# Delta-rule triangular solve as 64x64 products on quarters of the TensorE array, with TensorE's work of the delta stage in a written order

## Chip, cores, metric

One Trainium2 chip, one core. The metric is the device time of one execution in microseconds (us); the time shown of a kernel is the median of its runs.

## What is computed

A two-layer transformer-like block on 256 latent tokens and 256 context tokens of width 1024, in float32: modulation and norm, one input projection, three token mixers side by side (a gated convolution, a gated delta rule run in both directions, attention in a window of 128), an output projection, and a channel mixer: a dense SwiGLU in layer 0, a mixture of 8 experts in layer 1. The change touches the delta rule, which has 6 heads of 64 and runs over chunks of 64 tokens:

```python
a_mat = jnp.where(strict, jnp.einsum('bhcid,bhcjd->bhcij', kb, k) * decay, 0.0)
lmat = a_mat + jnp.eye(DN_CHUNK, dtype=F32)
rhs = jnp.concatenate([v * beta[..., None], kb * jnp.exp(gcum)[..., None]], axis=-1)
sol = lax.linalg.triangular_solve(lmat, rhs, left_side=True, lower=True, unit_diagonal=True)
...
v_new = u_c - jnp.einsum('bhik,bhkv->bhiv', w_c, s)
o = jnp.einsum('bhik,bhkv->bhiv', qg_c, s) + jnp.einsum('bhij,bhjv->bhiv', qk_c, v_new)
s = s * gl_c[..., None, None] + jnp.einsum('bhik,bhiv->bhkv', kd_c, v_new)
```

## The kernel before, in words

`layer` runs twice. In each layer `in_proj` makes the projections tile by tile; on the way `dn_gates` makes the gates (`sb` holds beta and -beta for each token and head), and `dn_units` cuts the delta rule into 8 units: a stream (context first, then latent), a direction, and a block of 128 tokens, which is two chunks of 64. For each pair of units `diag_inverse` inverts the 32x32 diagonal blocks of the triangular matrix, row by row, on VectorE for one direction and on GpSimd for the other, and writes the result to scratch in DRAM (`drz`, L1015).

`deltanet` is the delta stage. For each unit there are three parts:

- `dn_front` repeats the decay factors over heads (`headrep`, L769), for a block that is new also transposes keys and values and makes the key-query products (`dn_block`, L854 and L808), and builds the right-hand side `R` (L834, L835) and the operands `QD` (L838, L844).
- `dn_solve` reads the inverse `ud` from DRAM (L877, on SyncE's queue, two buffers), copies the off-diagonal blocks into `B` (L881, ScalarE), and makes three products (`prod`, L891): X = ud*R, then R = R - B*X, then Z = (ud*R)*beta. Each product has 6 matmuls, one for each head, of a 128x128 stationary tile that holds the two chunks as 64x64 blocks on its diagonal (the rest is zeros) and 128 columns. Three heads fill one PSUM tile; VectorE or ScalarE empties it (L896, L898; L900; L902).
- `dn_back` makes from Z the transition `gl` (L925, L934), `bb` (L931, L936), `er` (L943, L945), then the states of the two chunks one after the other (L961, L963) and the output (L972, L979, L985). `need_o` is false for the context in layer 1, whose output nobody needs: L943, L972 and L979 are left out there.

In layer 0 the matmuls of three modulation vectors (`mod_steps`, L316, weights of 1 MB each on SyncE's queue) are spread over the stage. The loop of `deltanet` issues front of unit i, back of unit i-1, solve of unit i and two steps of the modulation; a scheduler of the framework then puts the instructions of every engine and every queue into a static order by priority and by its own estimates, so matmuls of one product are often split and mixed with others, and work of the attention behind the stage (`mix_rest`) can come in front. PSUM has 8 banks; in this stage the tags f, b, c, x, m have 2, 2, 1, 2 and 1.

A matmul in float32 shows as two instructions in the trace: a product of 6 matmuls is a row of x12, one of 12 matmuls a row of x24.

Of the kernel before, what the change touches and what calls it, by code (L numbers as in the profile page):

```python
# [19 lines left out]
P = 128  # L20
# [147 lines left out]
class Build:  # L168
# [319 lines left out]
    def layer(self, l):  # L488
# [169 lines left out]
    def dn_gates(self, l, A):  # L658
# [20 lines left out]
        nc.vector.tensor_scalar(sb[:, :, :, 1], beta, -1.0, None, op0=OP.mult)  # L679
        pg = self.ps("p")  # L680
# [7 lines left out]
        self.D = dict(g=g, beta=beta, sb=sb, eg=eg)  # L688
# [21 lines left out]
    def deltanet(self, l):  # L710
# [8 lines left out]
        mods = itertools.chain(*[self.mod_steps(*m, "m") for m in self.MODS[l]])  # L719
        per = 2  # L720
        for i in range(9):
            if i < 8:
                self.dn_front(units[i])
            if i:
                self.dn_back(units[i - 1])
            if i < 8:
                self.dn_solve(units[i])
            for _ in range(per):
                next(mods, None)
        for _ in mods:  # L730
            pass
    def mix_rest(self, l, n, A, op):
# [3 lines left out]
        if l and not self.stop:  # L736
            self.router_open("m")
# [3 lines left out]
        if not self.stop == f"mix{l}":  # L741
            self.out_part(l, n, 0, [A["oc"][:, i] for i in range(2)] + [A["od"][:, i] for i in range(3)], op, "cm")
# [69 lines left out]
    def dn_front(self, U):  # L812
# [11 lines left out]
        pev = pe[:, :384].rearrange("p (a i) -> p a i", a=3)  # L824
        U["erl"] = dp.tile([P, 3, 2], F, name="erl", bufs=4)
        nc.scalar.activation(U["erl"], pev.rearrange("p q (c i) -> p q c i", c=2)[:, :, :, 0 if d else 63], AF.Copy)
        if need_o:
            U["er"] = dp.tile([P, 3, P], F, name="er", bufs=2)
            nc.vector.tensor_tensor(U["er"], pev, qk[:, :, 1, tk], op=OP.mult)
        if blk not in self.shared:  # L830
            self.shared[blk] = self.dn_block(A, tk, need_o)
# [14 lines left out]
    def dn_block(self, A, tk, need_o):  # L846
# [3 lines left out]
        out = []  # L850
        for i, src in enumerate((A["qk"][:, :, 0], A["v"])):
# [7 lines left out]
            else:  # L859
                nc.vector.tensor_copy(out[i], pv)  # L860
        kq = None
# [6 lines left out]
        return out + [kq]  # L868

    def dn_solve(self, U):  # L870
# [5 lines left out]
        R, ud, B = U["R"], dp.tile([P, 6, P], F, name="ud", bufs=2), self.bo[d]  # L876
        nc.sync.dma_start(ud, U["inv"])  # L877
# [6 lines left out]
        hs = [slice(0, 3), slice(3, 6)]  # L884

        def prod(lhs, rhs):
            for hh in hs:
                p = self.ps("b")
                v = p[:, :384].rearrange("p (a b) -> p a b", a=3)
                for i, m in enumerate(range(hh.start, hh.stop)):  # L890
                    nc.tensor.matmul(v[:, i, :], lhs[:, m, :], rhs[:, m, :], start=True, stop=True)  # L891
                yield v

        for hh, v in zip(hs, prod(ud, R)):
            if hh.start:
                nc.scalar.activation(X[:, hh, :], v, AF.Copy)  # L896
            else:
                nc.vector.tensor_copy(X[:, hh, :], v)  # L898
        for hh, v in zip(hs, prod(B, X)):
            nc.vector.tensor_tensor(R[:, hh, :], R[:, hh, :], v, op=OP.subtract)  # L900
        for i, (hh, v) in enumerate(zip(hs, prod(ud, R))):
            nc.vector.tensor_tensor(  # L902
                Z[:, hh, :].rearrange("p a (u k) -> p a u k", u=2), v.rearrange("p a (u k) -> p a u k", u=2),
                D["sb"][:, blk, d * 6 + 3 * i:d * 6 + 3 * i + 3, :][:, :, :, None].to_broadcast([P, 3, 2, 64]),
                op=OP.mult)

    def dn_back(self, U):
# [19 lines left out]
        for pr in range(3):  # L927
            for c in range(2):
                for par in range(2):
                    m = 2 * pr + par  # L930
                    nc.tensor.matmul(pbv[half[par], pr, c, :], qd[:, m, P + 64 * c:P + 64 * c + 64], Z[:, m, 0:64],  # L931
                                     start=pr == 0 and c == 0, stop=True, skip_group_check=True)
        glf = gl.rearrange("p a c k -> p a (c k)")
# [3 lines left out]
        if need_o:  # L937
# [7 lines left out]
            nc.vector.tensor_tensor(er, prv, er, op=OP.add)  # L945

        states = {}
        for c in ((1, 0) if d else (0, 1)):
# [7 lines left out]
            else:  # L956
# [6 lines left out]
                nc.vector.tensor_tensor(new, psv, bb[:, :, c, :], op=OP.add)  # L963
            self.st[d] = new
# [826 lines left out]
```

## Time and profile before

| | |
|---|---|
| median of 3 runs | 2018.47 us (2017.98 to 2021.39) |
| the profiled execution | 2015.34 us, span 2013.5 us, mean granted TensorE clock 0.974 |
| TensorE busy | 1907.0 us, 95% of the span |
| VectorE busy | 936.7 us, 47% |
| ScalarE busy | 577.4 us, 29% |
| GpSimd busy | 236.7 us, 12% |
| delta stage of layer 0, first to last solve | 220.4 to 323.4 us |
| delta stage of layer 1, first solve to the end of the last unit | 978.5 to 1071.5 us |

How to read it: the share of an engine over the span mixes stages with different limits. The first 1070 us hold projections, the two delta stages, attention and the dense layer; from then on the weights of the experts stream in. What the change is worth is read in the two delta stages, and then in whether the later stages pass it on.

### The profile page before, as it was taken

The page shows a single profiled execution, that of the slowest core. Times are in us where ns is not written, and L with a number is a line of the kernel's source. Part 1 is how long each engine was busy: PE and PEld are TensorE (multiplying, and loading weights), DVE is VectorE, ACT ScalarE, POOL GpSimd, SP SyncE. Part 2 cuts the span into 40 slices and gives each one's busy share as a digit, 9 for nine tenths or more (in the row PEclk, how much of TensorE's full clock was granted, in tenths as well). Part 3 has the DMA queues.
Part 4 walks back from the last instruction along what each step waited for, and adds up shares of the span by engine and source line. Part 5 has one row for each costly group of instructions (what it writes and reads, how often), then busy time and mean ns, then how long its engine had stood idle before and what let it go on. Part 6 is the DMA issues. An engine that isn't in the chain of part 4 may idle for free. (4 is left out here: it accounts for less than half of the span.)

```text
span 2013.5 us, 42986 instructions
## 1 busy us (share of the span) xinstructions
PE 1907.0 (95%) x17677; PEld 1476.4 (73%) x17677; DVE 936.7 (47%) x1862; ACT 577.4 (29%) x1075; POOL 236.7 (12%) x378
## 2 busy tenths in 40 slices
PE   6998999989999999898899999999999999999996
PEld 4776777667888888677786757885688767778853
DVE  3696665677655533577776411111012555521012
ACT  3742223453222223643225300000002354510001
POOL 1165101010000000034700000000000222200000
PEclk9999999999999999898899899999999999999998
DMA  7544453145445423235205799999999999999993
GB/s 302 161 99 108 141 172 131 48 164 188 155 169 209 167 79 105 79 80 142 63 25 207 286 409 408 407 406 408 401 407 406 403 406 406 400 408 397 391 408 135
DMA packets 186543, 497.79 MB, mean 247 GB/s; under 512 B 64864, under 2 KB 83424, under 8 KB 173792
## 3 DMA queue, kind: packets, MB, share of 16 engines
q1 hardware_dynamic: 186336, 494.94, 66.2%
q8 instruction: 141, 2.31, 0.5%
q14 instruction: 66, 0.54, 0.1%
HBM read 485.96 MB, written 8.91 MB: 246 GB/s over the span
## 5 line engine op out<-in xcount | busy, mean ns | idle before, releaser
L437 ACT ACTIVATE wh<-w 128x1024 fp32r<-128x1024 f32 (+4 forms) x162 | 141.6, 887 | 379.9 <-PE psx L467 196.7
L1655 PE MATMUL psx<-r,Xb 128*32 128x128 f32 x2016 | 227.8, 273 | 0.0
L1652 PE MATMUL psx<-r,Xb 128*32 128x384 f32 x2016 | 225.0, 487 | 1.4 <-DVE xs L1072 0.9
L438 DVE TENSOR_TENSOR wl<-w,wh 128x1024 fp32r<-128x1024 f32 (+4 forms) x162 | 163.0, 1014 | 118.1 <-ACT wh L437 117.7
L1655 PEld LDWEIGHTS psx<-r,Xb 128*32 128x32 f32 x2016 | 217.3, 110 | 0.6
L466 PE MATMUL psx<-xh,wh 128*128 128x512 f32 (+1 forms) x384 | 137.6, 387 | 13.0 <-ACT xh L437 8.0
L466 PE MATMUL psx<-fxh,wh 128*128 128x512 f32 x352 | 138.1, 394 | 4.9 <-ACT fxh L437 4.9
L468 PE MATMUL psx<-xh,wl 128*128 128x512 f32 (+1 forms) x384 | 131.8, 373 | 8.8 <-DVE wl L438 8.7
L467 PE MATMUL psx<-fxl,wh 128*128 128x512 f32 x352 | 137.5, 391 | 0.0
L468 PE MATMUL psx<-fxh,wl 128*128 128x512 f32 x352 | 137.3, 390 | 0.0
L467 PE MATMUL psx<-xl,wh 128*128 128x512 f32 (+1 forms) x384 | 132.9, 374 | 0.2 <-DVE xl L438 0.2
L1535 PE MATMUL psx<-r,Xb 128*64 128x256 f32 (+1 forms) x1792 | 130.9, 327 | 1.7 <-issue 1.7
L1732 ACT ACTIVATE hm<-psx 128x256 f32<-128x256 f32 (+3 forms) x63 | 26.2, 416 | 370.2 <-PE psx L1655 203.8
L1501 POOL TENSOR_TENSOR wlo<-r,whi 128x512 fp32r<-128x512 f32 x42 | 57.7, 1374 | 582.1 <-DMA r<-md 411.1
L1501 DVE TENSOR_TENSOR wlo<-r,whi 128x512 fp32r<-128x512 f32 x126 | 104.2, 857 | 44.0 <-ACT whi L1499 32.5
L1535 PEld LDWEIGHTS psx<-r,Xb 128*64 128x64 f32 (+1 forms) x1792 | 87.3, 123 | 41.6 <-issue 8.4
L1687 PE MATMUL psy<-r,hT 128*32 128x256 f32 (+1 forms) x672 | 112.7, 326 | 0.0
L1499 ACT ACTIVATE whi<-r 128x512 fp32r<-128x512 f32 x168 | 99.9, 630 | 42.5 <-PE psx L1508 21.2
L1684 PE MATMUL psy<-r,hT 128*32 128x384 f32 x1008 | 112.1, 486 | 0.0
L1772 PE MATMUL psy<-r,hT 128*32 128x256 f32 (+1 forms) x784 | 104.1, 472 | 1.5 <-DMA r<-md 0.8
L1733 DVE TENSOR_TENSOR hm<-hm,psx 128x256 f32<-128x256 f32 (+3 forms) x63 | 29.4, 466 | 148.5 <-PE psx L1655 75.8
L466 PEld LDWEIGHTS psx<-xh,wh 128*128 128x128 f32 x384 | 73.9, 199 | 29.6 <-ACT xh L437 8.9
(403 smaller groups left out, 3597.0 us busy)
## 6 DMA issues: line engine op xcount, KB each, us to landing
r<-mg SPq DMA_DIRECT2D x224, 512.0 KB, 10.1
r<-mu SPq DMA_DIRECT2D x224, 512.0 KB, 10.1
r<-md SPq DMA_DIRECT2D x224, 512.0 KB, 10.1
wm<-wmod SPq DMA_DIRECT2D x32, 1024.0 KB, 6.2
w<-win SPq DMA_DIRECT2D x24, 1024.0 KB, 5.5
w<-wgu SPq DMA_DIRECT2D x22, 1024.0 KB, 4.9
w<-wmod SPq DMA_DIRECT2D x16, 1024.0 KB, 6.9
w<-wdn SPq DMA_DIRECT2D x16, 704.0 KB, 4.0
```

The lines of the kernel that those rows point to most:

```text
L437: nc.scalar.activation(hi, src, AF.Copy)
L438: nc.vector.tensor_tensor(lo, src, hi.bitcast(F), op=OP.subtract)
L466: nc.tensor.matmul(out, wh[:, k, :], xh[:, k, :n], start=start and k == 0, stop=False)
L467: nc.tensor.matmul(out, wh[:, k, :], xl[:, k, :n], start=False, stop=False)
L468: nc.tensor.matmul(out, wl[:, k, :], xh[:, k, :n], start=False, stop=stop and k == kn - 1)
L1501: eng.tensor_tensor(wl, src, wh.bitcast(F), op=OP.subtract)
L1535: nc.tensor.matmul(out[m * j:m * j + m, :], x[:, k, :], w[k // 2][:, k % 2 * 512 + j * fw:k % 2 * 512 + (j + 1) * fw], start=k == 0, stop= ...
L1652: nc.tensor.matmul(out[32 * g:32 * g + 32], x[:, k, 32 * g:32 * g + 32], w[k // 2][:, c:c + 384], start=k == 0, stop=k == KT - 1, skip_gro ...
L1655: nc.tensor.matmul(out[96:, g * P:(g + 1) * P], x[:, k, 32 * g:32 * g + 32], w[k // 2][:, c + 384:c + 512], start=k == 0 and g == 0, stop= ...
L1684: nc.tensor.matmul(py[half][32 * g:32 * g + 32, :384], lhs[g], w[ft][:, 384 * half:384 * half + 384], start=first, stop=last, skip_group_c ...
L1687: nc.tensor.matmul(py[half][96:, o:o + n], lhs[g], w[ft][:, 768 + c:768 + c + n], start=first and o == 0, stop=last, skip_group_check=True)
L1772: nc.tensor.matmul(py[0][m * dq:m * dq + m, :dw], lhs, w[ft][:, dq * dw:(dq + 1) * dw], start=q == 0 and ft == 0, stop=q == 6 and ft == 3, ...
```

## The change

The two chunks of a head are no longer put on the diagonal of a 128x128 tile with zeros beside them. Each product has 12 matmuls of 64x64 stationary tiles with 128 columns. Even heads (`par` 0) use the quarters of the array whose rows and columns agree, odd heads (`par` 1) the two others, so that four successive matmuls address four different quarters. Even heads write one PSUM tile, odd heads another. For odd heads the result stands with the two chunks exchanged; `B` of odd heads is stored so that the second product exchanges them back, and Z is brought back in the multiplication with beta, by two instructions of 64 partitions with an exchanged copy of the factors, `sx`. The copies into `B` become four in place of two.

TensorE's order in `deltanet` is now the order of the code: in round i a step of the solve of unit i, one of the back of unit i-1 and one of the front of unit i+1 in turns, with two modulation steps in between. The other engines and the queues stay with the scheduler. `ud` is read in the front of a unit in place of its solve. PSUM's tag m is gone, its users take x (the modulation, the router's constants) or c (the output projection), and c has two banks.

```diff
@@ layer @@
-                with self.pool(f"at{l}", 2) as self.ap, self.psum(f"psx{l}", f=2, b=2, c=1, x=2, m=1):
+                with self.pool(f"at{l}", 2) as self.ap, self.psum(f"psx{l}", f=2, b=2, c=2, x=2):
@@ dn_gates @@
+        sx = one([4, 12, 2], "sx")
+        for c in range(2):
+            nc.vector.tensor_copy(sx[64 * c:64 * c + 64], sb[64 - 64 * c:128 - 64 * c])
@@ deltanet @@
-        mods = itertools.chain(*[self.mod_steps(*m, "m") for m in self.MODS[l]])
-        per = 2
-        for i in range(9):
-            if i < 8:
-                self.dn_front(units[i])
-            if i:
-                self.dn_back(units[i - 1])
-            if i < 8:
-                self.dn_solve(units[i])
-            for _ in range(per):
-                next(mods, None)
-        for _ in mods:
-            pass
+        mods = itertools.chain(*[self.mod_steps(*m, "x") for m in self.MODS[l]])
+        with self.tc.manual_schedule(engines={mybir.EngineType.PE}):
+            for i in range(-1, 9):
+                jobs = [f(units[j]) for f, j in ((self.dn_solve, i), (self.dn_back, i - 1), (self.dn_front, i + 1))
+                        if 0 <= j < 8]
+                more = 2
+                while jobs:
+                    jobs = [j for j in jobs if next(j, self) is not self]
+                    if more:
+                        next(mods, None)
+                        more -= 1
+            for _ in mods:
+                pass
@@ dn_front @@
+        U["ud"] = dp.tile([P, 6, P], F, name="ud", bufs=2)
+        nc.sync.dma_start(U["ud"], U["inv"])
...
-            U["er"] = dp.tile([P, 3, P], F, name="er", bufs=2)
+            U["er"] = dp.tile([P, 3, P], F, name="er", bufs=3)
...
+        yield
@@ dn_solve @@
-            p0 = 64 * c + BS * d
             o = BS * (1 - d)
-            nc.scalar.activation(B[p0:p0 + BS, :, 64 * c + o:64 * c + o + BS], U["at"][p0:p0 + BS, :, o:o + BS], AF.Copy)
+            for par in range(2):
+                p0, p1 = 64 * c + BS * d, 64 * (c ^ par) + BS * d
+                nc.scalar.activation(B[p1:p1 + BS, par::2, 64 * c + o:64 * c + o + BS], U["at"][p0:p0 + BS, par::2, o:o + BS],
+                                     AF.Copy)
...
-                for i, m in enumerate(range(hh.start, hh.stop)):
-                    nc.tensor.matmul(v[:, i, :], lhs[:, m, :], rhs[:, m, :], start=True, stop=True)
+            for pr in range(3):
+                for par in range(2):
+                    for c in range(2):
+                        i = half[c ^ par] if back else half[c]
+                        o = half[c] if back else half[c ^ par]
+                        m = 2 * pr + par
+                        nc.tensor.matmul(ps[par][o, pr, :], lhs[i, m, half[c]], rhs[i, m, :], start=pr == 0, stop=True,
+                                         skip_group_check=True)
...
+        for par, v in enumerate(prod(ud, R, False)):
+            sb = D["sx" if par else "sb"][:, blk, d * 6 + par:d * 6 + 6:2, :]
+            for c in range(1 + par):
+                i, o = (half[1 - c], half[c]) if par else (slice(0, P), slice(0, P))
+                n = 64 if par else P
+                nc.vector.tensor_tensor(
+                    Z[o, par::2, :].rearrange("p a (u k) -> p a u k", u=2), v[i].rearrange("p a (u k) -> p a u k", u=2),
+                    sb[i][:, :, :, None].to_broadcast([n, 3, 2, 64]), op=OP.mult)
```

How the orders move. The first place is TensorE in layer 0, solve of unit 3 (`psb`) with the back of unit 2 (`psc`) around it; before:

```order
L769 MATMUL psf<-cnorm,eg 64x128 x6
L925 MATMUL psc<-QD_1822,X 64x128 x6
L891 MATMUL psb<-R,ud 128x128 x4
L931 MATMUL psc<-X,QD_1822 64x64 x12
L891 MATMUL psb<-R,ud 128x128 x2
L891 MATMUL psb<-X,B_1816 128x128
L943 MATMUL psc<-QD_1822,X 64x128 x6
L891 MATMUL psb<-X,B_1816 128x128 x4
L961 MATMUL psc<-st_2004,gl 64x64 x6
L891 MATMUL psb<-X,B_1816 128x128
L891 MATMUL psb<-R,ud 128x128 x2
```

and now (L904 is the product, L944, L950, L963 and L982 are the former L925, L931, L943 and L961, L773 is the former L769):

```order
L904 MATMUL psb<-R,ud 64x128 x12
L944 MATMUL psc<-QD_1825,X 64x128 x6
L950 MATMUL psc<-X,QD_1825 64x64 x12
L773 MATMUL psf<-cnorm,eg 64x128 x6
L316 MATMUL psx<-w,sc 32x256 x8
L904 MATMUL psb<-X,B_1819 64x128 x12
L963 MATMUL psc<-QD_1825,X 64x128 x6
L861 MATMUL psf<-cnorm,tqk 128x128 x3
L316 MATMUL psx<-w,sc 32x256 x8
L904 MATMUL psb<-R,ud 64x128 x12
L982 MATMUL psc<-st_2156,gl 64x64 x6
```

Each product is one piece where it had been two or three, and the work between two products is fixed.

The second place is SyncE's queue in layer 1: the reads of the inverse (`ud`) of the 8 units and the writes of the last two inverses (`drz<-tt`). Before, and now:

```order
L877 DMA ud<-drz_530 128x6x128
L877 DMA ud<-drz_531 128x6x128
L877 DMA ud<-drz_530 128x6x128
L1015 DMA drz_533<-tt 48x16x32 x2
L1015 DMA drz_532<-tt 48x16x32 x2
L877 DMA ud<-drz_531 128x6x128
L877 DMA ud<-drz_532 128x6x128
```

```order
L830 DMA ud<-drz_533 128x6x128
L830 DMA ud<-drz_534 128x6x128
L1037 DMA drz_536<-tt 48x16x32
L1037 DMA drz_535<-tt 48x16x32 x2
L1037 DMA drz_536<-tt 48x16x32
L830 DMA ud<-drz_533 128x6x128
L830 DMA ud<-drz_534 128x6x128
L830 DMA ud<-drz_535 128x6x128
```

The third read, that of unit 2, stood ahead of the four writes and now stands behind them.

The third place is TensorE in layer 1, from the third product of unit 1 on; now:

```order
L904 MATMUL psb<-X,B_8142 64x128 x12
L982 MATMUL psc<-st_8337,gl 64x64 x6
L904 MATMUL psb<-R,ud 64x128 x24
L944 MATMUL psc<-QD_8146,X 64x128 x6
L950 MATMUL psc<-X,QD_8146 64x64 x12
```

The row of x24 is the third product of unit 1 and the first of unit 2, one behind the other; the back of unit 1 and all that follows stand behind them.

## Rows read from the trace of the kernel before

**Rows 1.** The page: busy time of the engines, and GB/s in 40 slices.
```profile
PE 1907.0 (95%) x17677; PEld 1476.4 (73%) x17677; DVE 936.7 (47%) x1862; ACT 577.4 (29%) x1075; POOL 236.7 (12%) x378
...
GB/s 302 161 99 108 141 172 131 48 164 188 155 169 209 167 79 105 79 80 142 63 25 207 286 409 408 407 406 408 401 407 406 403 406 406 400 408 397 391 408 135
```

**Rows 2.** Busy time by stretch, layer 0: us, engines, PEclk, DMA share, GB/s.
```profile
220.40:244.40 24.00, 24.00 (x267) 17.86 (x266) 19.16 (x41) 6.46 (x16) 1.09 (x2) 1.00 0.42 144
...
272.70:302.40 29.70, 29.70 (x386) 22.60 (x385) 22.20 (x47) 6.41 (x15) 0.83 (x1) 1.00 0.45 143
...
sum 103.00, PE 103.00 PEld 80.92 DVE 64.71 ACT 21.29 POOL 5.82; mean PE 25.75 PEld 20.23 DVE 16.18 ACT 5.32 POOL 1.46
```
(The five times are those of PE, PEld, DVE, ACT and POOL.)

**Rows 3.** The same view, layer 1: the start of the stage, and its units.
```profile
965.00:972.50 7.50, 0.54 (x5) 0.30 (x3) 6.84 (x19) 2.12 (x6) 6.87 (x14) 0.72 0.36 105
972.50:978.50 6.00, 5.99 (x31) 5.38 (x31) 1.74 (x4) 1.01 (x2) 5.92 (x9) 0.50 0.01 4
978.50:996.20 17.70, 17.49 (x160) 14.69 (x159) 13.72 (x35) 5.62 (x15) 14.43 (x32) 0.90 0.09 24
996.20:1015.90 19.70, 19.70 (x217) 16.50 (x216) 11.29 (x25) 5.02 (x13) 2.07 (x3) 1.00 0.36 81
1015.90:1036.10 20.20, 20.20 (x238) 17.04 (x237) 18.52 (x40) 6.13 (x14) 0.83 (x1) 1.00 0.08 21
```

**Rows 4.** TensorE in order of time, layer 0: start us, length, engine, line, tiles.
```profile
230.41 0.94 PE L808 MATMUL psf<-tqk 64*128 64x128 f32 x12
231.28 0.71 PE L891 MATMUL psb<-R,ud 128*128 128x128 f32 x4
...
255.45 0.83 PE L925 MATMUL psc<-QD,X 128*64 128x128 f32 x12
256.20 1.16 PE L891 MATMUL psb<-R,ud 128*128 128x128 f32 x8
257.29 0.92 PE L931 MATMUL psc<-X,QD 128*64 128x64 f32 x24
...
265.69 1.93 PE L316 MATMUL psm<-w,sc 128*32 128x256 f32 x32
267.55 0.65 PE L769 MATMUL psf<-cnorm,eg 128*64 128x128 f32 x6
...
272.71 1.60 PE L891 MATMUL psb<-R,ud 128*128 128x128 f32 x12
274.25 1.50 PE L316 MATMUL psm<-w,sc 128*32 128x256 f32 x24
...
283.17 0.92 PE L979 MATMUL psc<-er,st 64*64 64x64 f32 x24
284.01 0.63 PE L316 MATMUL psm<-w,sc 128*32 128x256 f32 x6
```

**Rows 5.** Groups of VectorE, 220.4 to 323.4 us: count, busy us, mean ns, idle before.
```profile
L900 DVE TENSOR_TENSOR R<-R,psb 128x384 f32<-128x384 f32 x16 | 8.8, 553 | 4.1 <-PE psb L891 3.7
L844 DVE TENSOR_TENSOR QD<-kq,E 64x384 f32<-64x384 f32 x16 | 8.8, 552 | 0.7 <-PE psc L972 0.4
L902 DVE TENSOR_TENSOR X<-psb,sb 128x384 f32<-128x384 f32 x15 | 8.4, 557 | 4.7 <-PE psb L891 4.3
```

**Rows 6.** SyncE's queue in layer 1: in time, its wait, and time to landing of `ud`.
```profile
995.85 2.28 SPq L1015 DMA_DIRECT2D drz<-tt  x4
998.24 37.28 SPq L877 DMA_DIRECT2D ud<-drz  x5
...
SPq L1015 <- POOL tt L1011: 8.8, 1, 8.8
...
DMA to landing us min/median/max: 3.3/3.6/6.4
```

**Rows 7.** TensorE in order of time, layer 1, around unit 2's first product.
```profile
994.77 0.94 PE L891 MATMUL psb<-R,ud 128*128 128x128 f32 x6
...
996.21 0.71 PE L891 MATMUL psb<-R,ud 128*128 128x128 f32 x4
```

More of the change, by code (lines that the diff above doesn't have):

```diff
@@ L687, in dn_gates @@
         nc.scalar.activation(eg, pg[:, :96].rearrange("p (k b h) -> p k b h", k=4, b=4), AF.Exp)
[L688 removed]
+        self.D = dict(g=g, beta=beta, sb=sb, sx=sx, eg=eg)
     def dn_units(self, l, A):
@@ L736, in mix_rest @@
         if l and not self.stop:
-            self.router_open("m")
+            self.router_open("x")
         for i, tag in enumerate(tags):
@@ L741, in mix_rest @@
         if not self.stop == f"mix{l}":
-            self.out_part(l, n, 0, [A["oc"][:, i] for i in range(2)] + [A["od"][:, i] for i in range(3)], op, "cm")
+            self.out_part(l, n, 0, [A["oc"][:, i] for i in range(2)] + [A["od"][:, i] for i in range(3)], op, "c")
     def dn_output(self, l, n, A):
@@ L827, in dn_front @@
         if need_o:
-            U["er"] = dp.tile([P, 3, P], F, name="er", bufs=2)
+            U["er"] = dp.tile([P, 3, P], F, name="er", bufs=3)
             nc.vector.tensor_tensor(U["er"], pev, qk[:, :, 1, tk], op=OP.mult)
+        yield
         if blk not in self.shared:
-            self.shared[blk] = self.dn_block(A, tk, need_o)
+            self.shared[blk] = []
+            yield from self.dn_block(A, tk, need_o, self.shared[blk])
         kn, vn, kq = self.shared[blk]
@@ L844, in dn_front, with dn_block @@
                 nc.vector.tensor_tensor(qd[half[c], :, half[c]], kq[half[c]], U["E"][half[c]], op=OP.mult)
-    def dn_block(self, A, tk, need_o):
+    def dn_block(self, A, tk, need_o, out):
         nc, dp, M = self.nc, self.dp, self.M
         half = [slice(0, 64), slice(64, P)]
-        out = []
         for i, src in enumerate((A["qk"][:, :, 0], A["v"])):
@@ L860, in dn_block @@
                 nc.vector.tensor_copy(out[i], pv)
+            yield
         kq = None
@@ L867, in dn_block @@
                     nc.vector.tensor_copy(dst, src)
-        return out + [kq]
+            yield
+        out.append(kq)
     def dn_solve(self, U):
@@ L875, in dn_solve @@
         half = [slice(0, 64), slice(64, P)]
-        R, ud, B = U["R"], dp.tile([P, 6, P], F, name="ud", bufs=2), self.bo[d]
-        nc.sync.dma_start(ud, U["inv"])
+        R, ud, B = U["R"], U["ud"], self.bo[d]
         for c in range(2):
-            p0 = 64 * c + BS * d
             o = BS * (1 - d)
-            nc.scalar.activation(B[p0:p0 + BS, :, 64 * c + o:64 * c + o + BS], U["at"][p0:p0 + BS, :, o:o + BS], AF.Copy)
+            for par in range(2):
+                p0, p1 = 64 * c + BS * d, 64 * (c ^ par) + BS * d
+                nc.scalar.activation(B[p1:p1 + BS, par::2, 64 * c + o:64 * c + o + BS], U["at"][p0:p0 + BS, par::2, o:o + BS],
+                                     AF.Copy)
@@ L882, in dn_solve @@
         X = dp.tile([P, 6, P], F, name="X", bufs=3)
         Z = U["Z"] = dp.tile([P, 6, P], F, name="X", bufs=3)
[L884 to L889, printed above, removed]
-                for i, m in enumerate(range(hh.start, hh.stop)):
-                    nc.tensor.matmul(v[:, i, :], lhs[:, m, :], rhs[:, m, :], start=True, stop=True)
-                yield v
@@ L894, in dn_solve, with prod @@
-        for hh, v in zip(hs, prod(ud, R)):
-            if hh.start:
-                nc.scalar.activation(X[:, hh, :], v, AF.Copy)
-            else:
[L898 to L905, printed above, removed]
+        def prod(lhs, rhs, back):
+            ps = [self.ps("b")[:, :384].rearrange("p (a b) -> p a b", a=3) for _ in range(2)]
+            for pr in range(3):
[6 more added lines that the diff above has]
+                                         skip_group_check=True)
+            return ps
@@ new lines, in dn_solve @@
+        for par, v in enumerate(prod(ud, R, False)):
+            if par:
+                nc.vector.tensor_copy(X[:, par::2, :], v)
+            else:
+                nc.scalar.activation(X[:, par::2, :], v, AF.Copy)
+        yield
+        for par, v in enumerate(prod(B, X, True)):
+            nc.vector.tensor_tensor(R[:, par::2, :], R[:, par::2, :], v, op=OP.subtract)
+        yield
+        for par, v in enumerate(prod(ud, R, False)):
+            sb = D["sx" if par else "sb"][:, blk, d * 6 + par:d * 6 + 6:2, :]
[5 more added lines that the diff above has]
+                    sb[i][:, :, :, None].to_broadcast([n, 3, 2, 64]), op=OP.mult)
@@ L932, in dn_back @@
                                      start=pr == 0 and c == 0, stop=True, skip_group_check=True)
+        yield
         glf = gl.rearrange("p a c k -> p a (c k)")
@@ L945, in dn_back @@
             nc.vector.tensor_tensor(er, prv, er, op=OP.add)
+            yield
         states = {}
@@ L963, in dn_back @@
                 nc.vector.tensor_tensor(new, psv, bb[:, :, c, :], op=OP.add)
+                yield
             self.st[d] = new
```

## The prediction

> **What bounds the kernel now.** I read the page first, then busy time by stretch in both delta stages, then TensorE in order of time, and last VectorE's groups and SyncE's queue. The page [rows 1] gives TensorE 95% of the span, but the GB/s slices show two regimes: up to slice 23 traffic is low and irregular, and from slice 24 on it stands at about 400 to 409, the stream of expert weights. The end of the kernel is that stream. What the change gains in a delta stage therefore counts only if the stream starts earlier. Its first buffers lie where the delta stage of layer 1 had its own, so I take a shift of that stage's end as a shift of the kernel's end, one to one.
>
> In layer 0 TensorE is busy for the whole stage, 103.00 us of 103.00, and VectorE for 64.71 [rows 2]. But VectorE is not idle everywhere: in the first two units it works 19.16 of 24.0 us, and 22.20 of 29.7 in the middle, where blocks are new. Layer 1 [rows 3] has the same picture (11.29 of 19.70 in one pair of units, 18.52 of 20.20 in the next), and ahead of it a hole: from 965.0 to 972.5 TensorE works 0.54 us, while GpSimd, busy 6.87 us, finishes an inverse and the memset of `B` that stands behind it. In the next 6 us the granted clock is 0.50 (the lower level, 1.2 GHz), and the mean after that 0.90. The reader is to keep this: a stand of 7 us costs more than 7 us.
>
> **Price of a product.** A product is 12 instructions of 128x128. Twelve in one piece took 1.54 us (272.71 to 274.25), eight took 1.09 (256.20 to 257.29) [rows 4]. The difference gives 0.112 us an instruction, and what is left is 0.19 us for a piece, the price of a change of tile shape. The 24 products of layer 0 are 288 instructions in 50 pieces (counted in the order): 288 x 0.112 + 50 x 0.19 = 42 us, 1.74 each.
>
> After, a product is 24 instructions of 64x64 with 128 columns. No row shows four quarters at once. Three rows bound it [rows 4]: two row halves together, into two banks, 12 in 0.87 us (L808); two column halves together, 12 in 0.75, 0.062 an instruction (L925); four column strips together, 32 instructions of 256 columns in 1.86, that is 0.058 each and 0.029 for 128 columns (L316). If four quarters work as four strips do, a product takes 24 x 0.029 + 0.17 = 0.87 us; if only two work at once, 24 x 0.062 = 1.5. I take 0.87, because both ways of pairing are seen and the new order addresses four quarters in succession. Even heads write one bank from two row halves. A row shows that this does not make instructions wait: L979 uses the two diagonal quarters into one bank, and 24 instructions of 64 columns took 0.84 us, 0.035 each, where one after the other they would take half of 0.112, 0.056 [rows 4]. The Trainium skill, "TensorEngine Tiling (Array Packing)", Restrictions and Gotchas, says the contrary: "Different row tiles cannot access same PSUM bank simultaneously". By that rule the product would stay at 1.5 us and the sum would be rival B's; the L979 row disagrees with it, at least where the two halves write different partitions, as here.
>
> So 1.74 - 0.87 = 0.87 us a product, 2.6 a unit. The written order also joins other pieces: 143 rows on TensorE between first and last solve before, 113 after of which 8 are attention, so 38 fewer; 26 of these are the products', already counted, and 12 x 0.2 = 2.4 us is 0.3 a unit. **2.9 us a unit** in TensorE's own work.
>
> **Added waits.** Before, the scheduler put other work wherever a product had to wait. Now what stands between two products is fixed. Both banks of the second product end together, so the two subtractions of R, 553 ns each [rows 5], run behind it: with some 0.3 us of signalling 1.4 us before the third product can start. Between stand the `er` product (L943 before), some 0.8 us, and in units 0 to 4 a modulation step. Z becomes three VectorE instructions in place of two. Half the partitions cost no less (L844 with 64 partitions 552 ns, L902 with 128 557 [rows 5]), so 0.55 us more a unit, on the path where the back of the unit waits for Z. Covered fully it is 0. Uncovered it is 1.4 for R, 0.85 for X and 3 x 0.55 + 0.3 for Z, 4.2 in all, less the 0.8 that always stands between: 3.4 us. I take 0.9 a unit (the uncovered rest of R, and half of Z's instruction), nearer to zero since every step has work of the back or the front beside it. Net 2.0 us a unit.
>
> **Layer 0.** Units 0 and 1 are near VectorE's bound (19.16 + 1.1 of 24.0), so I allow 2 us for the pair. Units 2 to 7 give 6 x 2.0 = 12. Eight pieces of attention now stand in the stage, and fill waits of units 5 to 7; that is worth some 2.5 us later. Sum -16.5.
>
> **Layer 1.** Here a queue matters. Before, the read of `ud` for unit 2 stands on SyncE ahead of the writes of the last two inverses. Now it stands behind. These writes wait 8.8 us for GpSimd; they are issued from 995.85, and the next read goes out at 998.24 [rows 6]. GpSimd doesn't get faster by this change. So unit 2's `ud` lands no earlier than 998.24 + 3.6 = 1001.8 (median from issue to landing), where unit 2's first product started at 996.21 before, with unit 1's from 994.77 ahead of it [rows 7]. It starts 5.6 us late. Because units 0 and 1 end 2 us earlier, TensorE stands 7 to 8 us: the back of unit 1 and all else is queued behind that product. As the hole at 965 did, such a stand should be followed by 6 us at half clock, which costs another 3: 8.6 us late at unit 3. Of the rest units 3, 6 and 7 gain 2.0 each, the pair in between is near VectorE's bound (18.52 of 20.20) and gains nothing, and attention in waits is again worth 2.5: 8.6 - 6 - 2.5 = 0.
>
> **At nothing.** The two copies of `sx` are 2 small VectorE instructions at the gates, beside projections. The copies into `B` become four: ScalarE works 21.29 of 103.00 us [rows 2], and `B` is filled a unit ahead; without that cover at most 0.7 us a unit. The third `er` buffer and the PSUM tags only take waits away. `ud` in layer 0 is read some 10 us ahead of its use.
>
> **Sum.** -16.5 us. The profiled execution took 2015.34, which gives 1998.8; the median of the runs is 3.1 above it, so I predict **2002.0** for the median. With w for the added waits of a unit the sum is 1.6 - 9 x (2.9 - w): nine units that gain, and 1.6 for all that doesn't depend on it (-2 - 2.5 + 8.6 - 2.5). At w = 0 this is 1994, at w = 1.8 it is 2010: the forecast's own range.
>
> **Rivals.**
>
> *B, two quarters at a time.* If row halves that share a bank do go one after the other, a product takes 1.5 us and a unit gains 3 x 0.24 + 0.3 = 1.0, of which waits take 0.9. Units 0 and 1 gain nothing: -2.5 + 8.6 - 2.5 - 9 x 0.1 = +2.7, 2021. For it: no row shows four quarters. Against it: L979's row.
>
> *C, no stand in layer 1.* If the inverse is finished earlier or the read reaches its place, layer 1 gains 2 + 6 + 2.5 = 10.5 and the time is 1991.5. For it: GpSimd's start may shift, since the stage before was also reordered. Against it: SyncE's order is static, and the writes stand ahead of the read.
>
> *D, slower: VectorE's delays reach TensorE.* In a fixed order each late eviction stops everything behind it, where before the scheduler had another piece at hand. Place: the third product behind the two subtractions, and the back behind Z. It decides once waits exceed 2.7 us a unit, where the formula gives zero; at the 3.4 worked out above it is +6.1, and 2 more as units 0 and 1 gain nothing: 2026.5. For it: VectorE at 80 to 90% in the units with new blocks. Against it: in the others it is near half.
>
> **How the numbers follow.** Forecast 0.63, B 0.10, C 0.13, D 0.14. The range goes from 1987 (C, with part of its waits covered as well) to 2021 (B); it leaves out D, and the ends of the others, 0.2 in all. 0.2% is 4 us. Faster: the forecast, C and a little of B and D, 0.77; the same, most of B and the edge of the forecast, 0.07; slower, D and the rest of B, 0.16.
>
> **What would show it.** Right: products as rows of x24 of about 0.87 us, instructions some 29 ns apart; the stage of layer 0 some 14 us shorter than 103, with VectorE's work nearly unchanged; Z in three VectorE instructions; in layer 1 a wait of 7 to 8 us of TensorE for `ud` at unit 2, SyncE waiting for GpSimd before it, and the lower clock after it. Wrong: products of 1.5 us (B); no wait for `ud` (C); TensorE idle by more than 2.7 us a unit behind VectorE (D); or an earlier end of the delta stage in layer 1 that the weight stream doesn't pass on.

## The result and the profile after

The changed kernel took 1993.61 us (median of 4 runs, 1991.60 to 1995.40), the kernel before in the same series 2018.22; the ratio is 0.9889, 95% interval [0.9872, 0.9906]. The medians differ by 24.6 us; the ratio stands for 22.4 us, and the spans of the two profiled executions differ by 21.9. 16.5 less had been forecast. The profiled execution took 1993.43 us. The sign and the size came out near the forecast. What the experiments change is the reason: which part of the change pays, and what holds layer 1.

The page of the profile, busy time and GB/s, against [rows 1]:

```profile
PE 1859.8 (93%) x18253; PEld 1438.2 (72%) x18253; DVE 944.5 (47%) x1882; ACT 583.7 (29%) x1107; POOL 236.1 (12%) x378
...
GB/s 305 159 102 108 194 183 90 55 209 191 148 158 190 169 73 108 85 97 121 49 26 231 346 409 408 408 406 409 403 397 408 404 403 408 407 407 397 382 408 140
```

TensorE works 47.2 us less, but only 21.9 us left the span (2013.5 to 1991.6): the rest is idle time. The expert stream starts earlier, as it should if the delta stage of layer 1 ends earlier: slice 23 has 346 GB/s in place of 286, and both kernels have 409 in slice 24.

Busy time by stretch, first product to last output, layer 0 and layer 1, of the kernel before and then of the changed one (PE, PEld, DVE, ACT, POOL; granted clock; DMA share; GB/s):

```profile
220.40:333.50 113.10, 113.10 (x1421) 86.94 (x1422) 68.25 (x143) 24.01 (x57) 5.82 (x7) 1.00 0.50 179
978.60:1071.30 92.70, 92.25 (x1063) 75.14 (x1064) 60.73 (x133) 24.70 (x60) 18.89 (x37) 0.98 0.13 31
```

```profile
221.00:319.30 98.30, 88.73 (x1713) 65.43 (x1714) 74.69 (x158) 28.87 (x77) 5.94 (x7) 1.00 0.55 196
959.30:1051.40 92.10, 78.26 (x1377) 60.77 (x1377) 69.39 (x148) 29.28 (x79) 18.74 (x38) 0.89 0.13 32
```

The length of a stretch minus its PE busy time is TensorE's idle time. In layer 0 TensorE never waited before (113.10 of 113.10) and waits 9.6 us now; the stage is 14.8 us shorter. In layer 1 it waits 13.8 us, the granted clock is 0.89 in the mean, and the stage is hardly shorter (92.7 and 92.1). What ends the waits of layer 1:

```profile
PE psb L904 <- DVE R L915: 4.4, 3, 2.2
PE psb L904 <- DMA ud<-drz: 3.7, 1, 3.7
PE psc L982 <- DVE st L984: 2.7, 2, 2.3
PE psb L904 <- DVE X L910: 1.7, 2, 0.9
```

TensorE in order of time: the first product of layer 1 before, and then, of the changed kernel, one product in layer 0, the first product of layer 1, and the start of its unit 2:

```profile
978.55 2.93 PE L891 MATMUL psb<-R,ud 128*128 128x128 f32 x12
```

```profile
246.51 0.89 PE L904 MATMUL psb<-X,B 64*64 64x128 f32 x24
247.33 0.88 PE L963 MATMUL psc<-QD,X 128*64 128x128 f32 x12
...
959.34 1.56 PE L904 MATMUL psb<-R,ud 64*64 64x128 f32 x24
...
976.93 2.01 PE L904 MATMUL psb<-R,ud 64*64 64x128 f32 x24 [2.19 <-DVE R L915]
982.62 1.67 PE L904 MATMUL psb<-R,ud 64*64 64x128 f32 x24 [3.68 <-DMA ud<-drz]
```

A product takes 0.82 us (246.51 to 247.33) where 0.87 was forecast. Unit 2's first product starts at 982.62 where it was 996.21 [rows 7], 13.6 us earlier. The first product of the stage is 19.2 us earlier (959.34 against 978.55), so this one place gives back 5.6 us, the forecast number. But TensorE stands twice, 2.2 us for R and 3.7 for `ud`, where one stand of 7 to 8 us for `ud` was forecast. The lower clock is there already behind the wait for R, ahead of the one for `ud`: the 24 instructions at 976.93 take 2.01 us, where they take 0.89 at 246.51. Some 45 us later it comes again, behind waits for VectorE:

```profile
976.90:987.60 10.70, 6.99 (x97) 5.94 (x97) 5.41 (x14) 3.30 (x9) 0.00 (x0) 0.54 0.49 104
987.60:1022.30 34.70, 28.97 (x558) 22.92 (x556) 30.42 (x64) 11.97 (x35) 2.49 (x3) 0.98 0.15 44
1022.30:1028.30 6.00, 5.94 (x84) 5.16 (x86) 3.94 (x9) 0.98 (x2) 0.83 (x1) 0.54 0.08 24
```

In the second stretch VectorE works 30.42 of 34.70 us: in these units it is near its bound. VectorE ahead of R's subtractions (L915) of 976.3 shows what R waits for:

```profile
973.88 1.11 DVE L846 TENSOR_TENSOR QD<-kv,eg 64x384 f32<-64x384 f32 x2
975.00 1.29 DVE L1068 TENSOR_REDUCE sm<-psx 128x1 f32<-128x512 f32 x2
976.32 1.02 DVE L915 TENSOR_TENSOR R<-R,psb 128x384 f32<-128x384 f32 x2
```

The next unit's QD and two reductions of the attention stand in front in VectorE's static order. TensorE's order is written, VectorE's is not.

### The profile page after: what moved, and what is told of

Same layout as the page of the kernel before. It is cut to its first block, busy times and chain, and to the rows that moved or that the text cites. A ratio compares the mean times of both kernels' runs of the same rounds, so it can differ in the third digit from the quotient of the medians.

```text
span 1991.6 us, 44165 instructions
## 1 busy us (share of the span) xinstructions
PE 1859.8 (93%) x18253; PEld 1438.2 (72%) x18253; DVE 944.5 (47%) x1882; ACT 583.7 (29%) x1107; POOL 236.1 (12%) x378
## 5 line engine op out<-in xcount | busy, mean ns | idle before, releaser
L466 PE MATMUL psx<-xh,wh 128*128 128x512 f32 (+1 forms) x384 | 137.7, 387 | 10.9 <-ACT xh L437 8.0
L468 PE MATMUL psx<-xh,wl 128*128 128x512 f32 (+1 forms) x384 | 133.0, 376 | 10.7 <-DVE wl L438 10.6
L1521 ACT ACTIVATE whi<-r 128x512 fp32r<-128x512 f32 x168 | 99.9, 630 | 42.7 <-PE psx L1530 19.2
```

The source lines that it names most:

```text
L466: nc.tensor.matmul(out, wh[:, k, :], xh[:, k, :n], start=start and k == 0, stop=False)
L468: nc.tensor.matmul(out, wl[:, k, :], xh[:, k, :n], start=False, stop=stop and k == kn - 1)
```

## Experiments

All times are medians; each ratio is to the kernel before in the same series, whose median drifted from 2018 to 2013 us between series, so kernels of different series are compared by ratios or by stages. "Idle" is length minus PE busy in the windows view of the stage (first product to last output). "Att." is TensorE's work for the attention that the scheduler put into the stage (added up from the trace, each instruction to the start of the next, idle time left out). It differs from kernel to kernel, so a shorter stage can also be one with less attention in it.

| kernel | us | ratio, 95% | layer 0: us, idle, att. | layer 1: us, idle, att. |
|---|---|---|---|---|
| before | | 1 | 113.1, 0.0, 5.5 | 92.7, 0.5, 8.8 |
| changed | 1993.61 | 0.9889 [0.9872, 0.9906] | 98.3, 9.6, 9.2 | 92.1, 13.8, 10.9 |
| quarters_only | 2009.83 | 0.9970 [0.9957, 0.9983] | 112.8, 2.4, 8.5 | 90.5, 4.5, 10.7 |
| order_only | 1994.37 | 0.9894 [0.9876, 0.9911] | 101.8, 2.1, 4.8 | 81.9, 1.6, 5.4 |
| tags_only | 2011.92 | 0.9978 [0.9965, 0.9992] | 108.0, 0.1, 2.6 | 84.8, 0.9, 4.1 |
| ud3 | 1993.83 | 0.9892 [0.9872, 0.9912] | 100.6, 9.3, 9.2 | 89.8, 10.5, 10.9 |
| mixed | 1983.35 | 0.9833 [0.9806, 0.9860] | 98.4, 9.6, 9.2 | 82.9, 1.4, 5.4 |
| relief | 1985.53 | 0.9842 [0.9815, 0.9869] | 92.4, 5.0, 9.1 | 88.6, 12.3, 13.2 |
| split_out | 2003.71 | 0.9947 [0.9919, 0.9975] | 107.3, 2.1, 5.5 | 85.5, 1.6, 6.5 |
| mixed_relief | 1975.14 | 0.9817 [0.9790, 0.9844] | 92.4, 5.0, 9.1 | 82.0, 1.7, 5.3 |
| twice_l1 | 1999.98 | 0.9931 [0.9910, 0.9953] | 98.5, 9.6, 9.2 | 100.3, 8.2, 13.1 |
| order_relief | 1992.06 | 0.9887 [0.9861, 0.9912] | 100.0, 1.7, 3.4 | 81.5, 1.0, 5.2 |

### The change taken apart: quarters_only, order_only, tags_only

quarters_only is the kernel before with `dn_solve` of the changed kernel (and `sx`). In that `dn_solve` the read of `ud` stays where it was, and the stops (`yield`) that cut the written order into steps are gone; against the changed kernel:

```diff
-        R, ud, B = U["R"], U["ud"], self.bo[d]
+        R, ud, B = U["R"], dp.tile([P, 6, P], F, name="ud", bufs=2), self.bo[d]
+        nc.sync.dma_start(ud, U["inv"])
...
-        yield
```

> The kernel before with the products on quarters alone (tiles, copies into B, sx, three instructions for Z); order of TensorE, PSUM tags and the read of ud as before. Theory 'price of the product' (24 products a layer from 1.68 to 0.88 us make the gain, the written order only keeps it): the stage of layer 0 loses 15 to 18 us of TensorE work, 5 to 8 us of it come back as waits, in both layers some -10 us each; 1995 to 2002. Rival 'written order' (the gain needs the order, since the scheduler splits and delays): less than 6 us of 24.6 gained, 2012 or more. Rival 'quarters pay all': 1994 or less.

order_only is the changed kernel with the old products:

```diff
...
-                        nc.tensor.matmul(ps[par][o, pr, :], lhs[i, m, half[c]], rhs[i, m, :], start=pr == 0, stop=True,
...
+                    nc.tensor.matmul(v[:, i, :], lhs[:, m, :], rhs[:, m, :], start=True, stop=True)
...
```

It also keeps the changed kernel's PSUM tags, the early read of `ud` and the third `er` buffer.

> The changed kernel with the products of the kernel before (128x128 tiles, two Z instructions, two copies into B); written order, PSUM tags, read of ud in the front as in the changed kernel. Theory 'price of the product': products in one piece at 1.54 in place of 1.68 us save 3 us a layer, waits in the fixed order cost about as much or more, and unit 2 of layer 1 still starts late: 2014 to 2024. Rival 'written order': more than half of the gain without quarters, 2006 or less.

tags_only is the kernel before with `psx` at f=2, b=2, c=2, x=2 and the users of m moved:

> The kernel before with the PSUM tags of the changed kernel alone (tag m gone, its users take x or c, c with two banks). Theory 'price of the product': no part of the gain, 2016 to 2020. Rival 'banks': the 5 us that came between the end of the delta stage and the end of layer 0's mixing came from a second bank c: 2010 to 2014.

My theory fell here. The written order with the old products gives the whole gain (0.9894 against 0.9889); the quarters under the scheduler's order give 0.3%. Of the other parts of order_only tags_only prices the tags, at 0.2%; the early read and the `er` buffer were not run by themselves; they can take waits away, and TensorE hardly waited in the stages of the kernel before (0.0 and 0.5 us). Both stages by the windows view in order_only:

```profile
223.50:325.30 101.80, 99.69 (x1402) 81.26 (x1401) 70.40 (x148) 25.81 (x63) 5.83 (x7) 1.00 0.53 190
969.50:1051.40 81.90, 80.34 (x1071) 70.31 (x1072) 61.88 (x134) 24.57 (x60) 19.85 (x39) 0.98 0.14 35
```

The products' groups in layer 0 say more, first the kernel before, then quarters_only, order_only and the changed kernel (count, busy us, mean ns, idle before):

```profile
L891 PE MATMUL psb<-R,ud 128*128 128x128 f32 x192 | 29.8, 290 | 0.0
L891 PE MATMUL psb<-X,B 128*128 128x128 f32 x96 | 14.8, 289 | 0.0
```

```profile
L899 PE MATMUL psb<-R,ud 64*64 64x128 f32 x384 | 23.2, 289 | 0.0
L899 PE MATMUL psb<-X,B 64*64 64x128 f32 x192 | 15.3, 298 | 0.1
```

```profile
L896 PE MATMUL psb<-R,ud 128*128 128x128 f32 x192 | 25.4, 282 | 0.0
L896 PE MATMUL psb<-X,B 128*128 128x128 f32 x96 | 12.8, 284 | 0.0
```

```profile
L904 PE MATMUL psb<-R,ud 64*64 64x128 f32 x384 | 17.1, 278 | 3.2 <-DVE R L915 3.1
L904 PE MATMUL psb<-X,B 64*64 64x128 f32 x192 | 7.6, 278 | 0.8 <-DVE X L910 0.8
```

Quarters without the order keep TensorE busy for 38.5 us, as much as whole tiles in the written order (38.2; before, 44.6); only both together come to 24.7. In these sums the time in which the pieces of two groups run side by side counts in both. Taken from each instruction to the start of the next it is 40.3 us before, 32.3 with the quarters alone, 36.4 with the order alone and 21.0 with both, so neither part alone gives half of it. The scheduler cut the 24 products of quarters_only into 68 pieces in layer 0 (counted in the trace, pieces of two products that touch taken as one; by this count 42 in the kernel before and 24 in order_only). 32 of the 68 stand behind a change of tile shape, as here:

```profile
301.32 0.45 PE L899 MATMUL psb<-R,ud 64*64 64x128 f32 x8
301.70 0.88 PE L937 MATMUL psc<-QD,X 128*64 128x128 f32 x12
302.50 0.65 PE L899 MATMUL psb<-R,ud 64*64 64x128 f32 x12
```

In layer 1 the stage is 10.2 us shorter with whole tiles than with quarters (81.9 against 92.1). 5.5 us of that is attention that does not stand in it.

tags_only was forecast at no change and gained 0.2%, by its time in the rival's range but not at the rival's place: from the end of layer 0's stage to the first product of layer 1 it takes 647.7 us, where the kernel before takes 645.1. Its stages are shorter, 113.1 to 108.0 and 92.7 to 84.8, with fewer changes of tile shape (107 and 80, counted, where the kernel before has 138 and 104). But 7.6 of these 13.0 us is attention that now stands outside the stages. Layer 1's stage ends 9.1 us earlier (1062.2 in place of 1071.3), and the span is only 3.1 us shorter: a shift of that end is not always a shift of the kernel's end, as the prediction took it.

### Is it the changes of tile shape? split_out

split_out is order_only with two kinds of the output's products, tiles of 128x64 and of 64x64, made in turns by pairs of heads:

```diff
         for pr in range(3):
             for par in range(2):
                 m = 2 * pr + par
                 nc.tensor.matmul(pov[half[par], pr, :], Z[:, m, 0:64], qd[:, m, 0:P], start=pr == 0, stop=False,
                                  skip_group_check=True)
-        for c in range(2):
-            if states[c] is None:
-                continue
-            for pr in range(3):
+            for c in range(2):
+                if states[c] is None:
+                    continue
...
```

> The kernel order_only with one edit: the first product of the output (128x64 tiles) and the products with the states (64x64 tiles) alternate by pairs of heads, 4 changes of tile shape more in each of the 12 units that have an output, the same matmuls. Theory 'changes of tile shape': 48 changes of 0.15 to 0.2 us on a TensorE that never waits: 7 to 10 us slower than order_only, 2001 to 2005. Rival 'what the order gives is overlap': the same instructions at the same places in the order, within 2 us of 1994.4.

2003.71 us, 9.3 above order_only. The stages grew by 5.5 and 3.6 us for 35 and 18 more changes (counted in the trace): 9.1 / 53 = 0.17 us each, or 0.14 without the 1.8 us of attention that came in besides. The rows give the same: the six pieces of an output follow each other by 0.37 us, 2.2 us in all, where the two whole pieces of order_only take 1.65 (1023.87 to 1025.52): 0.15 for each of four more changes. First split_out, then order_only:

```profile
308.78 0.44 PE L982 MATMUL psc<-QD,X 128*64 128x128 f32 x4
309.15 0.45 PE L988 MATMUL psc<-er,st 64*64 64x64 f32 x8
309.53 0.44 PE L982 MATMUL psc<-QD,X 128*64 128x128 f32 x4
```

```profile
1023.87 0.88 PE L982 MATMUL psc<-QD,X 128*64 128x128 f32 x12
1024.67 0.91 PE L989 MATMUL psc<-er,st 64*64 64x64 f32 x24
1025.52 1.60 PE L896 MATMUL psb<-R,ud 128*128 128x128 f32 x12
```

The written order has 89 and 64 changes in place of 138 and 104, 49 and 40 fewer. order_only takes 22.1 us off the two stages: TensorE works 25.3 us less and waits 3.2 more. At 0.14 to 0.17 us, 89 changes are 12 to 15 of the 25.3. Some 4 us more is attention that does not stand in the stages, and an estimated 1.3 modulation (160 of its instructions in layer 0's stage where there were 182, at 0.058 us each [rows 4]). The rest, 5 to 8 us, I have not traced, and the price of a change was measured between tiles of 128x64 and 64x64 only.

### Where quarters lose: mixed, twice_l1, ud3

mixed uses the quarters in layer 0 alone:

```diff
-                jobs = [f(units[j]) for f, j in ((self.dn_solve, i), (self.dn_back, i - 1), (self.dn_front, i + 1))
+                jobs = [f(units[j]) for f, j in ((self.dn_solve_full if l else self.dn_solve, i), (self.dn_back, i - 1), (self.dn_front, i + 1))
```

(`dn_solve_full` is the solve of order_only.)

> The changed kernel with the quarters in layer 0 only; in layer 1 the products are those of the kernel before (128x128 tiles), written order in both. Theory 'two layers, two signs': in layer 0 quarters shorten the stage by 5 us and what follows by 4 more against the written order alone, in layer 1 they lengthen it by 10 (92.1 against 81.9 us from first product to end). Then the parts add up: layer 1 from first product to end at 82 to 84 us, the kernel at 1983 to 1987. Rival 'end pinned by something else' (GpSimd's inverse, a transfer; both kernels ended the stage at 1051.4): the earlier start of layer 1 turns into waits and the time stays at 1991 to 1995.

1983.35 us: the layers add up. Layer 1 takes 82.9 us, and TensorE waits 1.4. SyncE's order differs here too, since the third read of `ud` stands ahead of the writes, as in order_only and in ud3 below, so that 82.9 is best held against ud3's 89.8. Of that difference 5.5 us is attention.

```profile
960.80:1043.70 82.90, 81.50 (x1071) 71.23 (x1072) 61.45 (x134) 24.57 (x60) 20.13 (x40) 0.97 0.14 35
```

twice_l1 makes each quarter product of layer 1 twice:

```diff
-            for pr in range(3):
+            for pr in [0, 1, 2] * (1 + U["l"]):
```

> The changed kernel with every product of layer 1 made twice in a row into the same banks (the same result), 24 x 0.65 = 16 us of TensorE work more, nothing else changed. Theory 'VectorE's queue and the evictions set the pace of layer 1': of the 16 us the 14 us of idle time take up the part that lies beside waits; the stage of layer 1 becomes 93 to 102 us in place of 92.1. Rival 'idle time costs by the clock': with TensorE busy the granted clock stays at the upper level through the stage and the stage gets shorter, 88 us or less, although more is computed.

```profile
959.20:977.00 17.80, 15.36 (x257) 11.77 (x258) 14.73 (x30) 4.31 (x11) 13.57 (x33) 0.83 0.13 19
977.00:1059.50 82.50, 76.75 (x1718) 62.84 (x1714) 57.05 (x121) 24.75 (x68) 5.68 (x6) 1.00 0.12 32
```

The clock stays at 1.00 from 977 on, so the rival saw that right; but the stage got longer, 100.3 us, as the theory had it. 16 us of work cost 8.2, of which 2.2 is more attention: the rest lay beside waits that are there anyway, or was paid back by the clock or by the wait for `ud`, which is gone here. A clock at its upper level alone does not make the quarters fast here. That the units go no faster than VectorE empties their banks fits this, but is not shown by it: a longer product also lengthens the chain from product to eviction to product.

ud3 gives `ud` a third buffer, by which unit 2's read goes ahead of the writes:

```diff
-        U["ud"] = dp.tile([P, 6, P], F, name="ud", bufs=2)
+        U["ud"] = dp.tile([P, 6, P], F, name="ud", bufs=3)
```

> The changed kernel with three buffers for ud in place of two, by which the read for unit 2 of layer 1 goes ahead of the writes of the last inverses on SyncE's queue. Theory 'the queue': the wait of 3.7 us for ud goes, and with it the 1.8 us that the lower clock took behind it; unit 2's first product starts up to 5.6 us earlier against the kernel before than now (977 in place of 982.6), the kernel ends at 1986 to 1989. Rival 'hidden by something else': unit 2 then waits for VectorE (R, Z of unit 1) or unit 4 for its own inverse as long, and the time stays within 2 us of 1993.6.

The read went ahead and the wait for `ud` is gone, but the time is the same, 1993.83: my theory missed. Layer 1's stage is 2.3 us shorter, and in this profile layer 0's is 2.3 longer at a clock of 0.97. So the wait is worth some 2 us of the stage; in the kernel's time the two intervals hide a gain of that size. The wait for R stays, and so does the low clock behind it:

```profile
980.81 1.61 PE L904 MATMUL psb<-R,ud 64*64 64x128 f32 x24 [2.19 <-DVE R L915]
982.68 0.69 PE L904 MATMUL psb<-R,ud 64*64 64x128 f32 x4 [0.26 <-DVE X L922]
983.93 1.55 PE L904 MATMUL psb<-R,ud 64*64 64x128 f32 x20 [0.55 <-DVE X L922]
```

### What they wait for: relief, order_relief, mixed_relief

relief takes work off VectorE:

```diff
-            nc.vector.tensor_tensor(qd[half[c], :, P + 64 * c:P + 64 * c + 64], kn[half[c]],
+            eng = nc.gpsimd if need_o and ui or ui > 2 else nc.vector
+            eng.tensor_tensor(qd[half[c], :, P + 64 * c:P + 64 * c + 64], kn[half[c]],
...
-                    nc.vector.tensor_copy(dst, src)
+                    nc.scalar.activation(dst, src, AF.Copy)
```

> The changed kernel with less on VectorE in the stage: the two QD multiplications by the end decay go to GpSimd (layer 0 from unit 1 on, layer 1 from unit 3 on), the four copies into kq to ScalarE. Theory 'VectorE's queue': the waits for R, X and st (7 us in layer 0, 9 in layer 1) come from work that stands ahead in VectorE's queue; with 1.1 us a unit and 1.4 us a new block less, 4 to 8 us less: 1986 to 1990. Rival 'chain of latencies': what counts is the product, its two evictions and the signals in a row, which stay; within 2 us of 1993.6.

1985.53 us, and the theory holds in layer 0: 98.3 to 92.4 us, the waits for R from 3.1 to 0.5. In layer 1 it holds less well: the stage is 3.5 us shorter, but the idle time is still 12.3, with 4.9 of it for `ud` and 6.9 for VectorE, where it had been 9.5:

```profile
PE psb L905 <- DMA ud<-drz: 4.9, 1, 4.9
PE psb L905 <- DVE R L916: 4.0, 4, 1.6
```

On GpSimd a QD multiplication takes 920 ns where VectorE needs 550; GpSimd had the time (5.94 busy of 98.3 us before the edit).

order_relief has the same edit on order_only, mixed_relief on mixed:

> The kernel order_only (written order, 128x128 products in both layers) with the relief of VectorE of the kernel relief. Theory 'a shorter product pays only where VectorE lets it': TensorE waits 2.1 and 1.6 us in the two stages of order_only, so there is little to relieve: 1990 to 1994, layer 0's stage at 100 to 102 us. The quarters of layer 0 are then worth 15 to 19 us against mixed_relief (1975.1) where they were worth 11 without the relief (1994.4 to 1983.4). Rival 'the relief pays by itself': 8 us or more less than order_only, 1986 or less.

> The kernel mixed (quarters in layer 0, 128x128 tiles in layer 1, written order in both) with the relief of VectorE of the kernel relief (two QD multiplications of a unit to GpSimd, copies into kq to ScalarE). Theory 'waits add up by layer': layer 0 as in relief (stage 92 us from first product to last output), layer 1 as in mixed (82.9 us) or a little less: 1974 to 1979. Rival 'the relief works only where TensorE waits, and it hurts where it doesn't' (in layer 1 GpSimd's slower QD would stall a TensorE that was 98% busy): layer 1 at 86 us or more, 1980 to 1985.

Whole tiles gain next to nothing by the relief (1992.06; 101.8 to 100.0 us in layer 0). With it the quarters are worth 100.0 - 92.4 = 7.6 us of layer 0's stage, without it 101.8 - 98.3 = 3.5, and each time the stage with quarters holds more attention besides (9.1 against 3.4 us, 9.2 against 4.8). The medians of order_only and mixed differ by more than the stage, 11 us. Of this the profiled executions show 5.6 (spans 1991.8 and 1986.2; the profiled one of mixed was its longest): 2.2 us ahead of the stage (it starts at 221.3 in place of 223.5), 3.4 in it and 3.1 up to layer 1's first product, less 3.1 from there on. The rest of the 11 us is in no trace. mixed_relief is the fastest, 1975.14 us, 0.9817; against order_relief the quarters of layer 0 are worth 17 us by the medians and 14 by the ratios, where 15 to 19 was expected. Its interval overlaps that of mixed, so between these two the stages decide: layer 0 98.4 to 92.4, layer 1 82.9 to 82.0.

```profile
218.60:311.00 92.40, 87.42 (x1715) 65.19 (x1714) 62.21 (x128) 33.83 (x93) 18.68 (x21) 1.00 0.58 209
950.50:1032.50 82.00, 80.26 (x1073) 70.39 (x1072) 55.42 (x116) 27.14 (x68) 28.93 (x49) 0.98 0.14 35
```

### Does sharing a bank cost? rowbank

rowbank gives each bank to one row half of the array:

```diff
-                        nc.tensor.matmul(ps[par][o, pr, :], lhs[i, m, half[c]], rhs[i, m, :], start=pr == 0, stop=True,
+                        nc.tensor.matmul(ps[c ^ par if back else c][o, pr, :], lhs[i, m, half[c]], rhs[i, m, :], start=pr == 0, stop=True,
```

> The changed kernel with the products' results sorted into the two PSUM banks by the row half of the array in place of the parity of the head: each bank is then written from one row half only (the heads' results stand in other places, so the evictions take mixed heads). Theory 'sharing a bank across row halves costs nothing where the partitions differ': 24 instructions stay at 0.82 us from first to next, 34 ns apart. Rival 'row halves of one bank wait for each other': a product falls towards 24 x 29 ns, 0.70 us.

```profile
249.19 0.89 PE L904 MATMUL psb<-X,B 64*64 64x128 f32 x24
250.00 0.88 PE L963 MATMUL psc<-QD,X 128*64 128x128 f32 x12
```

0.81 us, as with the shared bank (0.82): row halves that write different partitions of one bank don't wait for each other. The evictions are left as they were and take mixed heads, so rowbank does not compute the block's output; only the pace of its products is read, not its time. The rule that the prediction quotes from the Trainium skill, "TensorEngine Tiling (Array Packing)", Restrictions and Gotchas, would make the product 1.5 us; no run shows that here.

## Why the prediction was right, and where it was not

- **Price of a product: right.** 0.87 forecast, 0.82 measured in the row above, and 0.88 in the mean of layer 0 (21.0 / 24, to the start of the next instruction); rival B is out. It holds only in the written order: under the scheduler's the same instructions cost 1.35 us a product (32.3 / 24).
- **Share of the written order: too small**, and this is the step that failed. The sum has the pieces of the products in the price of the product, and 12 x 0.2 = 2.4 us is 0.3 a unit for all others. By its own terms the order is 0.9 us a unit (0.3, and 0.6 for 26 joined pieces of products) and the quarters 2.0. Without the attention, TensorE's work in layer 0's stage is 107.6 us before, 94.9 in order_only and 79.5 in the changed kernel: 1.6 a unit for the order, 1.9 for the quarters, 3.5 in place of 2.9. And the order keeps what it saves, since TensorE hardly waits in it (2.1 us), where in layer 0 half of what the quarters save turns into waits, and in layer 1 more than all of it. So the order alone takes 21 us off the kernel, as much as the whole change, and the quarters alone take off 6.
- **Added waits: right kind, too small.** 0.9 us a unit forecast; 9.6 / 8 = 1.2 in layer 0, and in layer 1 again 1.2 for VectorE (9.5 of the 13.8 us), with 3.7 us for `ud` besides. Most come from VectorE's static queue (R, st, X), as rival D had it, and with them the clock at 0.54 for 16.7 us of layer 1. The 0.3 us of signalling in the sum stands in none of its rows; here VectorE began 0.11 us behind a product (1027.50 to 1027.61) and TensorE 0.05 behind an eviction (1015.12 to 1015.17).
- **Layer 0: mechanism right, size off.** First to last product 103 to 89.5 us (14 forecast). But layer 1's first product starts 19.2 us earlier in place of 16.5: what follows the stage gained about 5, where 2.5 was put down.
- **Layer 1: right place, wrong worth.** The read behind the writes and the 5.6 us at unit 2 came as forecast, and the stage went from 92.7 to 92.1 us. But TensorE waits 3.7 us for `ud`, not 7 to 8, the low clock is there before that wait, and the sum puts 8.6 us on the two. ud3 takes the wait away and the stage gets 2.3 us shorter; the wait for R stays, and the low clock follows that. With whole tiles and the same early read the stage takes 82.9 us (mixed). What the quarters have more there is 9 us of waits, nearly all for VectorE, and 5.5 us of attention; how much each of them and the low clock cost is not taken apart. That the stage came out at zero is luck.
- **Sum.** Layer 0 with what follows 19.2 in place of 16.5, the rest 2.7 in place of 0, by the spans (2013.5 - 1991.6 = 21.9). The other 2.7 us to the 24.6 of the medians is the profiled execution of before, which was faster than its median. With the measured waits, 1.2 a unit, the formula of the sum gives 13.7 us: two terms that were too small, the order and the waits, stand against each other, and what follows layer 0's stage gained more than was put down. So the number is nearer than the reason, and in part by luck.

## What to carry to other kernels

Where matmuls of several tile shapes alternate, count the changes of shape in the trace and price them (0.14 to 0.17 us here) before pricing the matmuls: an order that keeps each product in one piece was worth as much as the whole change. A written order covers what is written: the scheduler still put attention into products of the changed kernel, 3 times in layer 0 and 7 in layer 1. When a stage gets shorter, look whether work of others has left it, as in tags_only. A shorter instruction on the bound engine pays only as far as the engines behind it follow: take the two parts apart, stage by stage, since one can help in one layer and hurt in the next (mixed). And when one engine's order is written by hand, read what the scheduler puts ahead of its partners in the other queues; moving 2 multiplications a unit to an idle engine, and 4 copies a new block to another, gave 6 us in layer 0.

## Not expected of the hardware

- Four quarters of the array run together from one instruction stream: 24 instructions of 64x64 with 128 columns took 0.82 us, 0.034 each, whether one bank is written from one row half or from both (rowbank).
- A change of tile shape between tiles of 128x64 and 64x64 costs 0.14 to 0.17 us (split_out).
- TensorE's idle time cost twice in layer 1: behind a wait of 2.2 us, with one of 3.7 soon after, and behind waits of 1.4 and 2.3 us, the granted clock was 0.54 for 10.7 and for 6.0 us (0.50 is 1.2 GHz). With the products doubled it was 1.00 from 977 us on.
